# Reordering the first transfers of an eight-core decoder-block kernel, and splitting the last tile's output stage into two halves of its tokens

## The chip, the cores and the metric

The kernel runs on the 8 cores of one Trainium2 chip. Each core works on one sequence of the batch of 8 and shares nothing with the others. The metric is device microseconds (us) of the slowest core.

In the profiles PE is TensorE (matmuls) and PEld its weight loads, DVE is VectorE, ACT is ScalarE, POOL is GpSimd, SP is SyncE, which issues most of the transfers; a q behind a name means the engine's sequencer. Cores 0 to 3 are one die of the chip, 4 to 7 the other; two neighbouring cores such as 2 and 3 are called a pair.

Executions come in two states. In the slow state the cores of one die, sometimes of both, have a lower granted clock in the records and the time is some per cent longer; this happens to both kernels and says nothing about them. A fast execution is **undisturbed** when every core's mean granted clock was above 0.985.

## The reference

```python
D_MODEL = 1024; BATCH = 8; SEQ = 4096; D_FF = 2816; EPS = 1e-6

def ada_rmsnorm(x, g, shift, scale):          # shift, scale: one vector per sequence
    return rmsnorm(x, g) * (1.0 + scale[:, None, :]) + shift[:, None, :]

def swiglu_ffn(h, w_in, w_out):
    gate, up = jnp.split(h @ w_in, 2, axis=-1)
    return (jax.nn.silu(gate) * up) @ w_out

def reference(x, c, w_mod, b_mod, ...):
    c_act = jax.nn.silu(c)
    mod = c_act @ w_mod[l] + b_mod[l]          # 9 vectors of 1024: shift, scale, gate of 3 sub-layers
    ...
    h = ada_rmsnorm(x, g_ffn1, sh1, sc1)
    x = x + 0.5 * gt1 * swiglu_ffn(h, w_ffn1_in, w_ffn1_out)
    h = ada_rmsnorm(x, g_mix, sh2, sc2)
    x = x + gt2 * mixing(h)                    # convolution group and recurrence group
    h = ada_rmsnorm(x, g_ffn2, sh3, sc3)
    x = x + 0.5 * gt3 * swiglu_ffn(h, w_ffn2_in, w_ffn2_out)
    return ada_rmsnorm(x, g_final, f_shift, f_scale)
```

All arrays are float32; the matrix products of the kernel are in bf16.

## The kernel before

A core's sequence is cut into 8 tiles of 512 tokens and held with features on the partitions, so a tile is 8 chunks of 128x512. Phase 1 does FFN 1 for pairs of tiles and stores the result. Phase 2 does mixing, FFN 2, the final norm and the store of `y`, tile by tile. Weights travel as slabs of 0.5 MB into a pool of 10 slots. In the first pair the 22 input slabs (`w1i`) are cast from f32 to bf16 by a GpSimd DMA on the way in and written back to a scratch copy in HBM, which later pairs load.

The program is a list of operations. A small list scheduler in Python, which simulates the engines with estimated durations, fixes one static order for each engine; at run time every engine goes through its list in order and waits for semaphores. Three arguments matter below: `prio` (smaller first), `after` (an order for the scheduler only, no wait on the chip) and `sync` (a real semaphore wait). All operations of one kind come from one helper, so the profile gives all matmuls line 443, all activations 401, all DMAs 450.

The parts that the change touches:

```python
def load_slab(nm, r, cast, prio=None, after=()):
    b = new(sl, f"{nm}{r}")
    if cast:
        src = dr(w_src[nm], r)
        dma("PL", lambda: b.ap, lambda: src, D_CAST, slot_sem(b, "PL"), [], [b], slab=True, prio=prio, after=after)
        d = scr[nm][r]
        dma("SP", lambda: d.ap, lambda: b.ap, D_SLAB, lambda: wb_sems[b.slot], [b], [d], prio=prio)
    # ... (else: load the bf16 slab from scratch)

P.prio = -24
mods(M_SC1, [None] * 8)        # 8 slabs of w_mod, each reduced on DVE against silu(c): scale of FFN 1
gs_op(M_SC1, V_G1)             # gs = g * (1 + scale)
P.prio = -20
mods(M_SH1, [None] * 8)        # shift of FFN 1

def norm(xs, msc, msh, after=(), prio=None):
    r = stats(xs, after, prio)             # squares, sums, two ones-matmuls on PE, r = 1/rms on ACT
    hb = []
    for f in range(8):
        t_ = new(p2, "nt")
        stt(lambda t_=t_: t_.ap, lambda f=f: xs[f].ap, gs[msc].ap[:, f:f + 1], lambda: r.ap, ALU.mult, ALU.mult,
            [xs[f], r, gs[msc]], [t_], after=after, prio=prio)                  # x * gs * r on DVE
        b = new(p1, "hb")
        # ... o, i = b, t_
        act(o, i, AF.Identity, [t_, modv[msh]], [b], dur=0.7, bias=modv[msh].ap[:, f:f + 1], prio=prio,
            alt=v_ts(o, i, modv[msh].ap[:, f:f + 1], ALU.add))                  # + shift, on ACT or DVE
        hb.append(b)
    return hb

# the pairs of phase 1
xss = [load_x(x_dr, t, prio=(-22 if t == 0 else -15) if pi == 0 else lp, after=prev_in[8 * (t % 2):8 * (t % 2) + 8]) for t in tiles]
hbs = [norm(xs, M_SC1, M_SH1, after=(last_in,), prio=300) for xs in xss]
for j in range(FC):
    slab = load_slab("w1i", j, pi == 0)
    ops = ffn_in(slab, hbs, hids, j)       # 8 + 8 matmuls per tile of the pair
    # ...
last_in = ops[-1]
# ... 12 output slabs, ffn_out per 3 of them, xmid stored

# the end of each tile in phase 2
for q in range(4):
    slabs = [load_slab("w2o", 3 * q + s, t == 0) for s in range(3)]
    ffn_out(slabs, q, [xs], [hid], gth[M_GT3])
r = stats(xs)
for f in range(8):
    b = xs[f]
    stt(...)                               # x * gs * r
    act(...)                               # + shift
    dma("PL", lambda d=d: d.ap, lambda b=b: b.ap, D_CHUNK, slot_sem(b, "PL"), [b], [d])   # y, from GpSimd

# the end of the program, on SP
replay(engs["SP"], h)
for smh, v in stores.items():
    h.wait_ge(smh.h, v)                    # every semaphore that a DMA ever raised
```

## Time and profile before

| | before |
|---|---|
| first runs, us | 2420.52, 2420.62, 2418.84 (and a slow one, 2465.01) |
| undisturbed runs in the later calls (chips 9, 5, 3), mean us | 2422.9, 2423.7, 2424.3 |
| span of the eight cores in the profiled run | 2409.5 to 2431.0 |
| time before the first FFN matmul (core 1) | 66.4 |
| last FFN matmul to the end (core 1) | about 23 |

The page of the profile, for the slowest core (core 1). The second line gives each engine's busy time, its share of the span and its instructions:

```profile
span 2431.0 us, 34520 instructions; the slowest of 8 cores (2409.5 to 2431.0 us)
...
PE 2317.3 (95%) x11168; PEld 1093.3 (45%) x11168; DVE 1180.9 (49%) x1975; ACT 920.8 (38%) x1394; POOL 115.1 (5%) x221
```

PE is the bound, but a 95% average hides where the other 5% lies. The windows view of before, core 1, cuts the span into stages; its first line names the columns:

```profile
core 1: us, PE busy (x) PEld busy (x) DVE busy (x) ACT busy (x) POOL busy (x), PEclk, DMA share, GB/s
0.00:66.40 66.40, 2.34 (x5) 0.45 (x5) 35.53 (x72) 23.38 (x35) 2.99 (x9) 1.00 0.98 270
66.40:220.00 153.60, 153.60 (x702) 69.20 (x703) 46.29 (x74) 33.24 (x55) 14.25 (x27) 1.00 0.96 207
220.00:240.00 20.00, 14.37 (x57) 5.96 (x56) 8.93 (x16) 8.33 (x13) 1.08 (x2) 0.83 0.96 282
240.00:2408.00 2168.00, 2146.43 (x10408) 1017.55 (x10405) 1083.32 (x1807) 847.24 (x1281) 92.47 (x175) 1.00 0.63 186
2408.00:2431.00 23.00, 0.60 (x3) 0.10 (x1) 6.83 (x10) 8.59 (x12) 4.31 (x8) 0.60 0.24 91
```

PE does almost nothing in the first 66.4 us, while the DMA engines are full (share 0.98): the head is a matter of which bytes come first. PE is then full. It stalls between 220 and 240. And it does almost nothing in the last 23 us, where DMA is mostly idle too (share 0.24): the tail is a chain of latencies.

What ends the head is in the timeline of before, core 1 (start, duration, engine, line, operation, tiles; in brackets the idle time before it and what ended that):

```profile
58.83 1.22 DVE L499 SCALAR_TENSOR_TENSOR sb_slab<-sb_slab,sb_crow 128x1024 f32<-128x1024 f32 x1 [1.77 <-DMA sb_slab<-wmod]
...
60.64 0.16 DVE L423 TENSOR_TENSOR sb_modv<-sb_modr,sb_vecs 128x8 f32<-128x8 f32 x1
60.72 8.03 DVE L419 SCALAR_TENSOR_TENSOR sb_c<-sb_c,sb_gs 128x512 f32<-128x512 f32 x12
60.90 7.34 ACT L401 ACTIVATE sb_h<-sb_c,sb_modv 128x512 bf16<-128x512 f32 x11 [9.56 <-DVE sb_modv L423]
...
66.40 8.94 PE L443 MATMUL ps<-sb_h,sb_slab 128*128 128x512 bf16 x30 [16.57 <-ACT sb_h L401]
```

The sixteenth and last modulation slab lands at 58.7 and its reduction starts at 58.83. Only then can the multiplies by `gs*r` and the activations run for the eight chunks, and PE begins at 66.40. In the records of DMA landings, x of tile 1 (2 MB) arrived from 33.4 to 47.3, ahead of the last six modulation slabs (48.6 to 58.7), though nothing needed it yet.

The stall near 228, from the PE timeline of the same core:

```profile
227.77 0.38 PE L443 MATMUL ps<-sb_h,sb_ones 128*128 128x512 bf16 x1
233.78 0.59 PE L443 MATMUL ps<-sb_h,sb_ones 128*128 128x512 bf16 x1 [5.63 <-DVE sb_h L423]
```

Matmuls with `sb_ones` sum squares over the partitions. Here they belong to tiles 2 and 3, whose x is still coming: PE's static order holds them in the middle of the first pair's work, so PE stands for 5.6 us.

And the tail, from the timeline of before, core 1:

```profile
2411.06 1.28 ACT L401 ACT_TABLE_LOAD   x1 [1.47 <-PE ps L443]
...
2413.13 0.63 ACT L401 ACTIVATE sb_c<-sb_c 128x512 f32<-128x512 f32 x1
2413.86 5.39 DVE L419 SCALAR_TENSOR_TENSOR sb_c<-sb_c,sb_gs 128x512 f32<-128x512 f32 x8 [3.41 <-ACT sb_c L401]
2414.71 5.36 ACT L401 ACTIVATE sb_c<-sb_c,sb_modv 128x512 f32<-128x512 f32 x8 [0.95 <-DVE sb_c L419]
2415.98 5.18 POOL L450 DMA_DIRECT2D y<-sb_c  x8 [104.39 <-ACT sb_c L401]
```

The last FFN matmul is at 2407.9. The reciprocal root is ready at 2413.8, the eight chunks are normalized and shifted one behind the other, and the eighth store is issued at 2420.6. But the span ends at 2431.0. The records of GpSimd, which the timeline does not print, show a DRAIN instruction of 10.18 us that begins with that last store and ends at 2430.8; it is there on all eight cores. The Trainium skill, "VectorE: DVE Perf Modes", section "The DRAIN you can't avoid", puts the DRAINs that the runtime adds around a kernel at about 12 ns on all engines. This one carries a line of the kernel, L862, where its last block begins, so it may be of another kind; it took some 850 times that, while SP's DRAIN at the same line took 0.01 us.

### The profile page before, as it was taken

How to read it: one execution, taken by the hardware profiler on the slowest of the kernel's cores; microseconds unless marked ns; L12 is line 12 of the kernel's file. 1: busy time of each engine (PE TensorE's matmuls, PEld its weight loads, DVE VectorE, ACT ScalarE, POOL GpSimd, SP SyncE). 2: the span in 40 equal slices, each digit the busy share in tenths (PEclk: the TensorE clock that was granted, in tenths of full speed). 3: DMA queues.
4: the chain of work that ended last, by engine and by line, in shares of the span. 5: the costliest groups of instructions: out<-in, count | busy, mean ns of one | idle time of the engine just before them, and what ended most of it. 6: DMA issues, size and time to landing. Idle time of an engine off the chain costs nothing.

```text
span 2431.0 us, 34520 instructions; the slowest of 8 cores (2409.5 to 2431.0 us)
## 1 busy us (share of the span) xinstructions
PE 2317.3 (95%) x11168; PEld 1093.3 (45%) x11168; DVE 1180.9 (49%) x1975; ACT 920.8 (38%) x1394; POOL 115.1 (5%) x221
## 2 busy tenths in 40 slices
PE   0999999999999999999899999999999999999996
PEld 0444444444444445454354454454454454454442
DVE  4513233523352337676285385484484574573322
ACT  2313111401130115556264364364364464473312
POOL 0100100010000000000000000000000000000000
PEclk9999999999999999999999999999999999999998
DMA  9899589768966755565976555555555555555551
GB/s 266 201 210 242 161 203 231 181 193 206 222 188 178 191 160 196 168 216 163 223 190 220 190 176 189 185 179 189 176 179 185 191 182 182 186 179 189 166 181 61
DMA packets 131711, 460.32 MB, mean 189 GB/s; under 512 B 16048, under 2 KB 16176, under 8 KB 130864
## 3 DMA queue, kind: packets, MB, share of 16 engines
q1 hardware_dynamic: 113184, 378.15, 48.8%
q0 software_dynamic: 18352, 79.97, 16.4%
q8 instruction: 94, 1.54, 0.3%
q14 instruction: 81, 0.66, 0.1%
HBM read 446.78 MB, written 79.69 MB: 217 GB/s over the span
## 4 chain that ended last, share of the span: by engine, by line
PE 84%; DMA 5%; SPq 4%; ACT 3%; issue 2%; DVE 2%; ACTq 0%; DVEq 0%; POOL 0%; POOLq 0%
PE ps L443 84%; SPq L450 4%; ACT sb_c L401 2%; DMA sb_c<-xmid 2%; DMA sb_c<-x 1%; DMA sb_slab<-wmod 1%; DMA sb_slab<-w2o 1%; DVE sb_c L734 0%; DVE sb_c L409 0%; ACT L401 0%; DVE sb_h L423 0%; ACT sb_h L401 0%; DVE sb_c L423 0%; DVE sb_c L419 0%; DVE sb_c L429 0%
## 5 line engine op out<-in xcount | busy, mean ns | idle before, releaser
L443 PE MATMUL ps<-sb_h,sb_slab 128*128 128x512 bf16 x9984 | 2176.7, 380 | 16.6 <-ACT sb_h L401 16.6
L443 PEld LDWEIGHTS ps<-sb_h,sb_slab 128*128 128x128 bf16 x9984 | 978.7, 98 | 1196.5 <-issue 28.0
L423 DVE TENSOR_TENSOR sb_h<-ps,sb_c 128x512 bf16<-128x512 f32 x352 | 240.7, 690 | 770.0 <-PE ps L443 728.3
L401 ACT ACTIVATE sb_c<-ps 128x512 f32<-128x512 f32 x400 | 237.7, 596 | 891.8 <-PE ps L443 891.4
L401 ACT ACTIVATE sb_c<-sb_c 128x512 f32<-128x512 f32 x332 | 204.4, 627 | 294.3 <-DVE sb_c L419 194.9
L401 ACT ACT_TABLE_LOAD x102 | 130.9, 1283 | 219.3 <-PE ps L443 195.9
L419 DVE SCALAR_TENSOR_TENSOR sb_c<-ps,sb_gth,sb_c 128x512 f32<-128x512 f32 x128 | 94.9, 749 | 216.6 <-PE ps L443 215.9
L423 DVE TENSOR_TENSOR sb_c<-sb_c 128x512 f32<-128x512 f32 x224 | 149.1, 687 | 88.3 <-ACT sb_c L401 85.8
L419 DVE SCALAR_TENSOR_TENSOR sb_c<-sb_c,sb_gs 128x512 f32<-128x512 f32 x256 | 173.5, 746 | 32.6 <-ACT sb_c L401 32.5
L443 PE MATMUL ps<-sb_ub,sb_slab 128*128 128x256 bf16 x1024 | 115.0, 273 | 4.9 <-DVE sb_c L409 4.4
L401 ACT ACTIVATE sb_h<-sb_c,sb_modv 128x512 bf16<-128x512 f32 x160 | 105.1, 716 | 20.5 <-DVE sb_c L419 10.3
L499 DVE SCALAR_TENSOR_TENSOR sb_slab<-sb_slab,sb_crow 128x1024 f32<-128x1024 f32 x88 | 107.0, 1217 | 11.9 <-DMA sb_slab<-wmod 11.3
L443 PEld LDWEIGHTS ps<-sb_ub,sb_slab 128*128 128x128 bf16 x1024 | 99.6, 98 | 21.9 <-issue 8.1
L443 PE MATMUL ps<-sb_h,sb_ones 128*128 128x512 bf16 x96 | 34.8, 391 | 71.6 <-DVE sb_h L423 71.0
L450 POOL DMA_DIRECT2D y<-sb_c x64 | 34.5, 540 | 1124.1 <-ACT sb_c L401 974.9
L423 DVE TENSOR_TENSOR sb_h<-sb_c 128x512 bf16<-128x512 f32 x96 | 65.3, 688 | 25.4 <-ACT sb_c L401 23.3
L419 DVE SCALAR_TENSOR_TENSOR sb_c<-sb_ux,sb_vecs,sb_c 128x512 f32<-128x512 f32 x96 | 69.5, 745 | 1.7
L419 DVE SCALAR_TENSOR_TENSOR sb_c<-ps,sb_modv,sb_c 128x512 f32<-128x512 f32 x64 | 47.9, 749 | 32.4 <-PE ps L443 32.4
L419 DVE SCALAR_TENSOR_TENSOR sb_ub<-sb_c,ps 64x256 bf16<-64x256 f32 x128 | 53.8, 420 | 15.1 <-PE ps L443 11.7
L450 POOL DMA_DIRECT2D xmid<-sb_c x64 | 34.8, 544 | 360.0 <-DVE sb_c L419 358.3
L401 ACT ACTIVATE sb_c<-sb_c,sb_lam 128x512 f32<-128x512 f32 x64 | 50.0, 821 | 0.5
L443 PEld LDWEIGHTS ps<-sb_h,sb_ones 128*128 128x128 bf16 x96 | 9.0, 98 | 88.8 <-issue 81.9
(51 smaller groups left out, 508.7 us busy)
## 6 DMA issues: line engine op xcount, KB each, us to landing
sb_slab<-b_w2i SPq DMA_DIRECT2D x176, 512.0 KB, 3.7
sb_slab<-wmod SPq DMA_DIRECT2D x88, 512.0 KB, 5.9
sb_slab<-b_w2o SPq DMA_DIRECT2D x84, 512.0 KB, 3.5
sb_slab<-b_w1i SPq DMA_DIRECT2D x66, 512.0 KB, 6.0
sb_slab<-b_win SPq DMA_DIRECT2D x64, 512.0 KB, 4.4
sb_slab<-b_dcw SPq DMA_DIRECT2D x64, 512.0 KB, 3.5
sb_slab<-b_w1o SPq DMA_DIRECT2D x36, 512.0 KB, 5.2
sb_c<-x SPq DMA_DIRECT2D x64, 256.0 KB, 10.7
```

The source lines that it names most:

```text
L401: return A("ACT", dur, lambda: (lambda o, i: (lambda h: [h.activation(out=o, in_=i, func=func, bias=bias, scale=scale)]))(out(), in_()), r ...
L419: return A("DVE", dur, lambda: (lambda o, a, b: (lambda h: [h.scalar_tensor_tensor(out=o, in0=a, scalar=scalar, in1=b, op0=op0, op1=op1)]) ...
L423: return A("DVE", dur, lambda: (lambda o, a, b: (lambda h: [h.tensor_tensor(out=o, in0=a, in1=b, op=op)]))(out(), in0(), in1()), reads, wr ...
L443: return [h.matmul(o, lhsT=l, rhs=r, start=(first and i == 0), stop=(last and i == n - 1)) for i, (l, r) in enumerate(pr)]
L450: lambda: (lambda o, i: (lambda h: [h.dma_start(out=o, in_=i)]))(out(), in_()),
L499: return lambda h: [h.scalar_tensor_tensor(out=w, in0=w, scalar=1.0, in1=crow.ap, op0=ALU.mult, op1=ALU.mult, accum_out=o)]
```

## The change

Two independent parts.

The **head**: x of tile 0 goes first, then the sixteen modulation slabs of FFN 1, then x of tile 1. Casts 0 and 1 of `w1i` wait for modulation reductions, cast 2 for the fourth chunk of x of tile 1, and casts from 3 on for its last chunk. The norm is regrouped, so that DVE multiplies x by r (which needs no modulation) and ACT applies scale and shift in one activation. The first matmul group is split per chunk, so that it starts with the first chunk. The mixer's gate weights are loaded later, and so are the eight modulation slabs of FFN 1's gate, whose place moves from behind the second `w1i` slab to behind the ninth (not in the cuts below).

The **tail**: the last tile does its output matmuls, the sum of squares, the final norm and its stores for the first 256 tokens and then for the other 256, and issues those stores from SP instead of GpSimd. This costs twelve more loads of output slabs.

```diff
-        def load_slab(nm, r, cast, prio=None, after=()):
+        def load_slab(nm, r, cast, prio=None, after=(), sync=()):
 # ... sync goes to the cast's dma; mods() returns its last reduction and records all in mod_ops
-                stt(lambda t_=t_: t_.ap, lambda f=f: xs[f].ap, gs[msc].ap[:, f:f + 1], lambda: r.ap, ALU.mult, ALU.mult,
-                    [xs[f], r, gs[msc]], [t_], after=after, prio=prio)
+                tt(lambda t_=t_: t_.ap, lambda f=f: xs[f].ap, lambda: r.ap, ALU.mult, [xs[f], r], [t_], prio=prio, after=after)
 # ...
-                act(o, i, AF.Identity, [t_, modv[msh]], [b], dur=0.7, bias=modv[msh].ap[:, f:f + 1], prio=prio,
-                    alt=v_ts(o, i, modv[msh].ap[:, f:f + 1], ALU.add))
+                act(o, i, AF.Identity, [t_, modv[msh], gs[msc]], [b], dur=0.72, bias=modv[msh].ap[:, f:f + 1],
+                    scale=gs[msc].ap[:, f:f + 1], prio=prio,
+                    alt=v_ts(o, i, gs[msc].ap[:, f:f + 1], ALU.mult, modv[msh].ap[:, f:f + 1], ALU.add))
 # ... ffn_in(split=True): the gate group's 8 matmuls as 8 operations; ffn_out and stats take a width
-            xss = [load_x(x_dr, t, prio=(-22 if t == 0 else -15) if pi == 0 else lp, after=prev_in[8 * (t % 2):8 * (t % 2) + 8]) for t in tiles]
-            hbs = [norm(xs, M_SC1, M_SH1, after=(last_in,), prio=300) for xs in xss]
+            if pi == 0:
+                xss = [load_x(x_dr, t, prio=-26 if t == 0 else -15, after=[None if t == 0 else sh1_last] * 8) for t in tiles]
+                hbs = [norm(xs, M_SC1, M_SH1, prio=-23 if t == 0 else 300) for t, xs in zip(tiles, xss)]
 # ... (else: as before)
-                slab = load_slab("w1i", j, pi == 0)
-                ops = ffn_in(slab, hbs, hids, j)
+                slab = load_slab("w1i", j, pi == 0, sync=() if pi else (mod_ops[M_SH1 + 2 * j] if j < 2 else xss[-1][3 if j == 2 else 7].lw,),
+                                 after=[xb.lw for xb in xss[-1]] if pi == 0 and j >= 2 else ())
+                ops = ffn_in(slab, hbs, hids, j, split=(j == 0))
 # ...
+            last = t == n_tiles - 1
+            for cs in ([slice(0, T)] if not last else [slice(0, T // 2), slice(T // 2, T)]):
+                # ... the four groups of ffn_out, stats, final norm on w = 256 columns
+                    e = "SP" if last else "PL"
+                    dma(e, lambda d=d: d.ap, o, D_CHUNK * w / T, slot_sem(b, e), [b], [d])
 # ...
-        loads.sort(key=lambda o: use[o.writes[0]])
+        loads.sort(key=lambda o: (min(o.prio, 0), use[o.writes[0]]))
```

## The prediction

> **What bounds it now.** The page gives PE 95% of a 2431.0 us span, at 0.99 of its clock. The windows put 2.3 us of PE work into the first 66.4 us and 0.6 into the last 23; in between PE idles about 27 us of 2342. So the steady part is PE-bound (0.217 us per 512-column matmul); the change attacks the 66 us head and the 23 us tail.
>
> **Head before.** The timeline shows the sixteenth modulation slab (scale and shift of FFN 1) landing at 58.7, because x of tile 1 (2 MB) and four weight casts went before it with DMA saturated (share 0.98, 270 GB/s). Then come the last reduction and eight chained multiply/activation pairs (0.67 us each) before the first matmul at 66.4.
>
> After: constants (landing 7.5 as now), x of tile 0 (0.86 us per chunk: done near 15), sixteen slabs (1.63 us each in the trace: near 41, near 45 with two casts let in). The multiply by 1/rms no longer needs the modulation, so only activations remain behind it, and the first group starts per chunk. First FFN matmul estimated at 47-49, about 18 us earlier.
>
> Not all stays won. Until x of tile 1 has landed (about 54) and is normalized (61-65), PE has only tile 0: about 3.4 us per slab, with casts 2 and up held behind x of tile 1, landing from about 57. I expect about 5 us of starvation, plus a cold restart (first matmuls take 0.43 us; the Trainium skill, "TensorE: Matmul & The Clock Gate", Part 1, says PE falls to half clock after an idle window of about 3.4 us; the trace agrees: slow after the head and after the 5.6 us gap at 228). Net head gain about 13 us. From 100 to 240 us DMA share is about 1.0 and x of tile 3 lands at 236, where PE already waits 5.6 us. PE will arrive there earlier than DMA can, so I take off 3 us: 10 remain.
>
> **Tail before.** Timeline: last FFN matmul 2407.9, reciprocal root ready 2413.8 (with a 1.28 us table load), last store issued 2420.6, landed 2423.9, end 2431.0. The GpSimd drain behind the last store takes 10.2 us on every core, and ends the span.
>
> After: half the columns, table already loaded: root ready 2.8 us after the last matmul, eight chunks 3.5-4 us, stores from SP, so the GpSimd drain runs long before. SP then walks about 120 semaphore waits at 0.05 us. End about 13.5 us after the last matmul instead of 23.4. Halving costs PE little (256-column matmuls are 0.110 us), but twelve more 0.5 MB slabs are loaded: 24 at 1.6 us each in 39 us, just enough with 9 prefetched; perhaps 1 us lost. Tail gain about 9.5 us.
>
> **Elsewhere.** DVE 0.746 becomes 0.69 per norm multiply; off the path.
>
> **Prediction.** 2420.6 - 10 - 9.5 = about 2401 us; range 2391 to 2411. Faster by over 2% (48 us) exceeds what head and tail can give: 0.01. Within 2%: 0.98. Slower: 0.01.
>
> **What would show it.** First FFN matmul before 50; a PE gap of several us between 53 and 66 ending on a DMA or on the activations of tile 1; casts landing from about 57; wait on stats of tiles 2/3 near 210-225 as long as before or longer; last matmul to end 13-15 us; no GpSimd drain in the end chain.
>
> **What would make it wrong.** Casts held so late that PE starves through several slabs (head gain under 5); casts arriving so smoothly that all 18 us stay (2393); the stall near x of tile 3 growing to 15 us; slab starvation in the last tile; a rearranged static order moving the mid-kernel gaps.

## The result

The fast runs of the changed kernel took 2407.28, 2410.0 and 2412.54 us, against 2420.52, 2420.62 and 2418.84 before. A ratio is computed as the mean time of one kernel's fast runs over that of the other's of the same rounds, so it is not quite the ratio of the medians. Here it is 0.9958, with a 95% interval of 0.9936 to 0.9981: faster by about 10 us. Three of the changed kernel's six runs fell in the slow state and are left out.

The page of after, for its slowest core (core 0):

```profile
span 2405.7 us, 35029 instructions; the slowest of 8 cores (2386.8 to 2405.7 us)
...
PE 2318.5 (96%) x11346; PEld 1110.4 (46%) x11346; DVE 1183.6 (49%) x2019; ACT 931.4 (39%) x1394; POOL 111.2 (5%) x213
```

PE's busy time is the same within 1.2 us. What changed lies in its idle time. The windows of after, core 0, cut at the corresponding places (columns as above):

```profile
0.00:45.70 45.70, 1.17 (x2) 0.21 (x2) 31.77 (x68) 11.16 (x16) 1.42 (x6) 1.00 0.95 281
45.70:62.00 16.30, 10.57 (x38) 4.15 (x39) 9.31 (x17) 10.04 (x15) 3.71 (x7) 0.92 1.03 238
62.00:210.00 148.00, 148.00 (x678) 66.65 (x677) 46.14 (x74) 34.70 (x57) 12.19 (x23) 0.99 1.00 217
210.00:230.00 20.00, 16.86 (x71) 7.26 (x70) 11.19 (x19) 10.85 (x17) 1.08 (x2) 0.91 1.00 330
230.00:2391.00 2161.00, 2141.68 (x10562) 1032.06 (x10559) 1081.12 (x1836) 859.82 (x1283) 92.85 (x175) 1.00 0.64 190
2391.00:2405.70 14.70, 0.27 (x1) 0.10 (x1) 4.06 (x11) 4.86 (x10) 0.00 (x0) 0.61 0.22 72
```

The head is 20.7 us shorter and the tail 8.3 us shorter, but a new stage with 5.7 us of idle PE has appeared behind the head (16.30 less 10.57), and the stall near x of tile 3 is still there (20.00 less 16.86 is 3.1 us idle, against 20.00 less 14.37, 5.6, before). The end of the head, in the timeline of after, core 0:

```profile
43.20 1.23 DVE L500 SCALAR_TENSOR_TENSOR sb_slab<-sb_slab,sb_crow 128x1024 f32<-128x1024 f32 x1 [2.07 <-DMA sb_slab<-wmod]
...
44.54 0.17 DVE L423 TENSOR_TENSOR sb_modv<-sb_modr,sb_vecs 128x8 f32<-128x8 f32 x1
44.81 2.22 ACT L401 ACTIVATE sb_h<-sb_c,sb_modv,sb_gs 128x512 bf16<-128x512 f32 x3 [24.88 <-DVE sb_modv L423]
```

The sixteenth slab now lands at 43.05, and 2.6 us after its reduction began PE starts. The PE timeline of after shows the start and the new gap:

```profile
45.76 8.73 PE L443 MATMUL ps<-sb_h,sb_slab 128*128 128x512 bf16 x32 [28.68 <-ACT sb_h L401]
54.33 0.38 PE L443 MATMUL ps<-sb_h,sb_ones 128*128 128x512 bf16 x1
57.48 0.38 PE L443 MATMUL ps<-sb_h,sb_ones 128*128 128x512 bf16 x1 [2.77 <-DVE sb_h L423]
60.76 19.47 PE L443 MATMUL ps<-sb_h,sb_slab 128*128 128x512 bf16 x77 [2.90 <-DMA sb_slab<-w1i]
```

With two slabs cast, PE does 32 matmuls of tile 0, then waits 2.8 us for the squares of tile 1 and 2.9 us for the third slab, which landed at 60.6. Later, in the same view of after:

```profile
215.61 0.38 PE L443 MATMUL ps<-sb_h,sb_ones 128*128 128x512 bf16 x1
219.13 0.38 PE L443 MATMUL ps<-sb_h,sb_ones 128*128 128x512 bf16 x1 [3.14 <-DVE sb_h L423]
```

And the tail, in the timeline of after, core 0:

```profile
2393.07 0.47 ACT L401 ACTIVATE sb_c<-ps,sb_cst 128x256 f32<-128x256 f32 x1 [1.11 <-PE ps L443]
2393.64 0.42 ACT L401 ACTIVATE sb_c<-sb_c 128x256 f32<-128x256 f32 x1
2394.16 2.77 DVE L423 TENSOR_TENSOR sb_c<-sb_c 128x256 f32<-128x256 f32 x8 [1.60 <-ACT sb_c L401]
2394.67 3.55 ACT L401 ACTIVATE sb_c<-sb_c,sb_modv,sb_gs 128x256 f32<-128x256 f32 x7 [0.62 <-DVE sb_c L423]
2395.34 3.77 SPq L450 DMA_DIRECT2D y<-sb_c  x8
```

No table load and no long GpSimd DRAIN at the end any more: in the records that DRAIN now begins at 2293, a hundred microseconds before the end, and still lasts 10.7 us (10.3 to 11.5 over the eight cores). The last store is issued at 2398.72 and lands at 2400.50. SP does not stand still for that landing: its records show 121 closing semaphore waits, about 0.05 us apart, from 2399.16 to 2405.49, with a single pause of 0.35 us.

One profile is one core of one execution, so I also read from each trace, as a mean over its fully recorded cores (in e1_again below without core 3, which had the lower clock), when the n-th matmul with weights was executed. The 352nd is past the head, the 760th is past the stall at x of tile 3:

| us, mean of cores | 1st | 352nd | 760th | last | last to end |
|---|---|---|---|---|---|
| before | 66.3 | 144.1 | 238.6 | 2396.5 | 23.4 |
| after | 45.1 | 132.1 | 227.2 | 2385.1 | 15.2 |

From the 760th to the last matmul both take 2158 us (2157.9 and 2158.0): in these two executions the middle of the kernel neither wins nor loses, and everything is in the head and in the tail. (Over all the traces below this stretch runs from 2154.7 to 2163.7, so a difference of a few us in it needs more than one trace.)

### The profile page after: what moved, and what is told of

Same layout as the page of the kernel before. It is cut to its first block, busy times and chain, and to the rows that moved or that the text cites. A ratio compares the mean times of both kernels' runs of the same rounds, so it can differ in the third digit from the quotient of the medians.

```text
span 2405.7 us, 35029 instructions; the slowest of 8 cores (2386.8 to 2405.7 us)
## 1 busy us (share of the span) xinstructions
PE 2318.5 (96%) x11346; PEld 1110.4 (46%) x11346; DVE 1183.6 (49%) x2019; ACT 931.4 (39%) x1394; POOL 111.2 (5%) x213
## 4 chain that ended last, share of the span: by engine, by line
PE 87%; DMA 6%; ACT 3%; DVE 2%; issue 2%; SPq 1%; ACTq 0%; DVEq 0%; POOLq 0%
PE ps L443 87%; DMA sb_c<-x 2%; ACT sb_c L401 2%; DMA sb_c<-xmid 2%; SPq L450 1%; DMA sb_slab<-wmod 1%; DVE sb_c L423 1%; DMA sb_slab<-w1i 0%; DVE sb_c L749 0%; DVE sb_c L409 0%; ACT L401 0%; DVE sb_h L423 0%; DVE sb_c L419 0%; DVE sb_ub L419 0%; DVE sb_c L429 0%
## 5 line engine op out<-in xcount | busy, mean ns | idle before, releaser
L443 PE MATMUL ps<-sb_h,sb_slab 128*128 128x512 bf16 (+1 forms) x10160 | 2178.2, 376 | 31.8 <-ACT sb_h L401 28.9
L443 PEld LDWEIGHTS ps<-sb_h,sb_slab 128*128 128x128 bf16 x10160 | 995.9, 98 | 1195.9 <-issue 44.6
L423 DVE TENSOR_TENSOR sb_c<-sb_c 128x512 f32<-128x512 f32 (+1 forms) x492 | 308.8, 672 | 115.6 <-ACT sb_c L401 113.0
L401 ACT ACTIVATE sb_c<-sb_c 128x512 f32<-128x512 f32 (+1 forms) x329 | 198.5, 616 | 263.0 <-DVE sb_c L419 183.3
L419 DVE SCALAR_TENSOR_TENSOR sb_c<-ps,sb_gth,sb_c 128x512 f32<-128x512 f32 (+1 forms) x136 | 96.7, 717 | 212.0 <-PE ps L443 211.6
L401 ACT ACTIVATE sb_h<-sb_c,sb_modv,sb_gs 128x512 bf16<-128x512 f32 x151 | 108.9, 801 | 38.5 <-DVE sb_modv L423 24.9
L423 DVE TENSOR_TENSOR sb_h<-sb_c 128x512 bf16<-128x512 f32 (+1 forms) x98 | 65.8, 678 | 21.8 <-ACT sb_c L401 19.6
L443 PE MATMUL ps<-sb_h,sb_ones 128*128 128x512 bf16 (+1 forms) x98 | 34.4, 382 | 37.3 <-DVE sb_h L423 37.0
L419 DVE SCALAR_TENSOR_TENSOR sb_ub<-sb_c,ps 64x256 bf16<-64x256 f32 x128 | 53.8, 420 | 15.1 <-PE ps L443 11.6
L409 DVE TENSOR_SCALAR sb_c<-ps,sb_vecs 64x256 f32<-64x256 f32 x85 | 40.7, 484 | 8.9 <-ACT sb_c L401 4.7
L401 ACT ACTIVATE sb_c<-sb_c,sb_modv,sb_gs 128x512 f32<-128x512 f32 (+1 forms) x65 | 43.6, 751 | 1.2 <-DVE sb_c L423 1.2
```

The lines of the kernel that those rows point to most:

```text
L401: return A("ACT", dur, lambda: (lambda o, i: (lambda h: [h.activation(out=o, in_=i, func=func, bias=bias, scale=scale)]))(out(), in_()), r ...
L409: f = lambda: (lambda o, a: (lambda h: [h.tensor_scalar(out=o, in0=a, scalar1=s1, scalar2=s2, op0=op0, op1=op1)]))(out(), in0())
L419: return A("DVE", dur, lambda: (lambda o, a, b: (lambda h: [h.scalar_tensor_tensor(out=o, in0=a, scalar=scalar, in1=b, op0=op0, op1=op1)]) ...
L423: return A("DVE", dur, lambda: (lambda o, a, b: (lambda h: [h.tensor_tensor(out=o, in0=a, in1=b, op=op)]))(out(), in0(), in1()), reads, wr ...
L443: return [h.matmul(o, lhsT=l, rhs=r, start=(first and i == 0), stop=(last and i == n - 1)) for i, (l, r) in enumerate(pr)]
```

## The experiments

The question is small: the prediction was 2401 us, the fast runs took about 2410. Two candidate reasons: either the head gives back more than I took off (at the new gap, or at x of tile 3), or the tail was mis-sized. Twelve runs were made, two of them of the change unaltered, on three chips, each call with its own runs of before. "Mean core" is the mean span over the cores of the undisturbed runs; it scatters less than the slowest core does (standard deviation from run to run 0.8 to 2.5 us), so a difference of 1 us in the last column is not resolved.

| run | chip | ratio of fast runs [95%] | undisturbed: us (runs) | before, same chip | mean core less before's |
|---|---|---|---|---|---|
| e1_again | 9 | 1.0004 [0.9973, 1.0035] | 2411.3 (2 of 6) | 2422.9 | -12.5 |
| e2_head_only | 9 | 1.0018 [0.9979, 1.0056] | 2418.4 (3 of 6) | 2422.9 | -4.7 |
| e3_tail_only | 9 | 0.9974 [0.9959, 0.999] | 2416.9 (5 of 6) | 2422.9 | -5.4 |
| e4_sp_stores | 9 | 0.9987 [0.997, 1.0004] | 2420.3 (4 of 7) | 2422.9 | -2.4 |
| e5_warm | 5 | 0.9941 [0.9929, 0.9954] | 2409.6 (5 of 6) | 2423.7 | -13.1 |
| e6_no_hold | 5 | 0.9952 [0.9938, 0.9967] | 2412.3 (5 of 6) | 2423.7 | -11.9 |
| e7_order_only | 5 | 0.9948 [0.9935, 0.9962] | 2409.9 (5 of 6) | 2423.7 | -14.2 |
| e8_waits | 5 | 0.9931 [0.9917, 0.9944] | 2407.0 (4 of 6) | 2423.7 | -16.4 |
| e9_late_stats | 3 | 0.9916 [0.9888, 0.9944] | 2406.4 (6 of 6) | 2424.3 | -18.2 |
| e10_combo | 3 | 0.9888 [0.986, 0.9916] | 2399.8 (6 of 6) | 2424.3 | -24.8 |
| e11_control | 3 | 0.9938 [0.9903, 0.9973] | 2411.7 (4 of 7) | 2424.3 | -13.0 |
| e12_best | 3 | 0.9854 [0.9819, 0.9889] | 2391.3 (5 of 6) | 2424.3 | -30.2 |

The runs that are missing from the fourth column were slow or had a pair of cores at a lower clock. All twelve gave correct results. The times of the matmuls in the traces:

| us, mean of cores | 1st | 352nd | 760th | 352nd to 760th | last to end |
|---|---|---|---|---|---|
| e1_again | 44.7 | 131.7 | 227.0 | 95.4 | 15.2 |
| e2_head_only | 43.8 | 132.1 | 228.2 | 96.1 | 23.4 |
| e3_tail_only | 65.0 | 143.1 | 236.3 | 93.2 | 15.8 |
| e4_sp_stores | 65.5 | 143.4 | 234.0 | 90.6 | 20.3 |
| e5_warm | 45.0 | 130.8 | 227.9 | 97.1 | 15.2 |
| e6_no_hold | 44.7 | 128.7 | 226.0 | 97.2 | 15.2 |
| e7_order_only | 47.1 | 131.5 | 224.2 | 92.8 | 15.4 |
| e8_waits | 45.6 | 131.8 | 225.8 | 94.0 | 10.5 |
| e9_late_stats | 45.4 | 131.4 | 219.5 | 88.1 | 15.7 |
| e10_combo | 44.7 | 130.7 | 218.8 | 88.1 | 10.7 |
| e11_control | 44.8 | 131.5 | 226.7 | 95.1 | 15.2 |
| e12_best | 47.5 | 132.1 | 220.2 | 88.1 | 11.3 |

### e1_again: the change unaltered, timed in rounds

No edit.

> The changed kernel unaltered, timed again with more rounds and with the per-core spans of both kernels. Theory A (the traces are right: about 11.5 us won by the head and 8.3 us by the tail on every core, so the mean core is about 20 us shorter; the 10 us first timed come from few fast runs and from the slowest of eight cores, which scatters by 10 us): mean core span 18 to 21 us below that of the kernel before, slowest core 13 to 22 us below, ratio about 0.992 to 0.9945. Theory B (half of the gain is given back in the middle of the kernel, where the static order was rearranged, and the profiled run of the kernel before was an unusually slow one): ratio stays at 0.9955 to 0.9965 and the mean core span is only about 10 us shorter.

The ratio of fast runs is 1.0004, which seems to say that the change is worth nothing. The cores say otherwise. In four of the six runs two neighbouring cores (2 and 3, or 6 and 7, or 0 and 1) have a mean clock of 0.98 and a span 20 to 30 us longer than the rest. In the profiled run these are cores 2 and 3, at 0.983 and 0.981, with spans of 2421.5 and 2429.5 us; the other six take 2390.2 to 2407.2. The windows view of e1_again, core 3 (columns as above):

```profile
77.00:215.00 138.00, 138.00 (x527) 57.18 (x526) 33.15 (x52) 20.32 (x34) 10.55 (x20) 0.81 0.92 211
```

and the same stretch of the same execution on core 4:

```profile
77.00:215.00 138.00, 137.37 (x629) 62.54 (x640) 43.84 (x69) 29.37 (x50) 12.13 (x23) 1.00 1.00 228
```

Core 3 does 527 matmuls where core 4 does 629, with PE busy all the time on both: its clock was granted at 0.81. In the clock records the value is 0.8125, for 162 us, beginning 4.2 us after the clock had come back from the half-rate window behind the head (4.8 us on core 2). The Trainium skill, "TensorE: Matmul & The Clock Gate", Part 1, section "Seeing it yourself", describes a limiter that takes a whole die to 13/16 of its clock while three or more of its cores run dense matmuls, and holds it there. The level agrees (13/16 is 0.8125). The extent does not: here it is a pair, for 162 us, and in undisturbed runs all eight cores run dense matmuls at a mean clock of 0.99.

With the pair's runs set aside, two runs remain: 2411.3 against 2422.9 us, and a mean core 12.5 us shorter. Neither theory had that: it is far below the 18 to 21 us of theory A, which took the two first traces at their word, and little above the 10 us of theory B. Is the pair's lower clock a cost of the change, since its head is followed by a half-clock window in the gap at 54 to 61? On this chip it looked so: four of six runs here, three in e2_head_only, none in ten runs of before. But on chip 5, four kernels with the new head showed no such pair in their fast runs, two of them (e7_order_only, e8_waits) with the same half-clock window; and on chip 3 one run of before had it (2444.72 us, cores 2 and 3 at 0.982 and 0.983). So the change is not needed for it. What brings it on stays open.

### e2_head_only and e3_tail_only: one part at a time

```diff
 # e2_head_only: the change, but
-            last = t == n_tiles - 1
+            last = False
```

```diff
 # e3_tail_only: before, but with the change's stats, ffn_out and end of the tile
+            last = t == n_tiles - 1
+            for cs in ([slice(0, T)] if not last else [slice(0, T // 2), slice(T // 2, T)]):
+                # ... ffn_out, stats, final norm and SP stores per half, as in the change
```

> Only the head part (order of transfers, held casts, norm without the scale in its multiply, per-chunk first group); the last tile in one piece, stored by GpSimd. Theory A: first FFN matmul near 44.7 us, 352nd slab matmul about 12 us earlier than in the kernel before, last matmul to end 23.4 us as before; time 11 to 12 us below before (ratio 0.9953). Theory B: the head is won, but the middle gives back about as much, so the ratio is 0.998 or nearer to 1 and the distance from the 1056th to the last matmul grows by 5 us or more.

> Only the tail part (last tile in two halves, stores from SP) on the kernel before. Theory A: first FFN matmul near 66 us as before, last matmul to end 15.1 us in place of 23.4 us, time 8 us below before (ratio 0.9966). Theory B (the tail is worth less, because the second set of output slabs or the half-width matmuls slow PE): last matmul about 3 us or more later than in the kernel before, ratio 0.998 or nearer to 1.

In the times, the head alone takes 4.7 us off the mean core and the tail alone 5.4; together 10.2, against 12.5 to 13.0 for the whole change. Both are below what theory A of their expectations had (11 to 12 us and 8 us off the slowest core, where 4.5 and 6.0 came). The two parts add up, roughly, as parts at the two ends of a program should. In the traces, the tail alone has the old head (1st matmul at 65.0) and the new end (15.8), and the head alone the new head (43.8) and the old end (23.4).

The traces also give sizes, larger ones. Over the three kernels with the old head (before, e3, e4) the 352nd matmul is at 143.5 on average, and over four with the new one (after, e1, e2, e11) at 131.8: the head wins 11.7 us by then. At the 760th it is 236.3 against 227.3: 9.0. So 2.7 us are given back between the two, at x of tile 3. The last chunk of that x lands at 232.4 before and 222.2 after (mean over the cores); it did not become earlier by as much as PE did. The 2.7 is no firmer than its traces: from the 352nd to the 760th the three with the old head take 94.5, 93.2 and 90.6 us.

In the tail, last matmul to end falls from 23.4 to 15.2, which is 8.2 us, but the last matmul itself comes later: from the 10000th to the last it is 218.0 us before and 219.4 after (218.0 in e2, which has the old end, and 219.4 in e3). Halving costs 1.4 us on PE. Net 6.8.

The sum of 9.0 and 6.8 is 15.8, and the timed gain is 11.6 to 13.0. The record says where most of the other 3 us are likely to lie: in traces of executions that were long or short for their kernel. Against the undisturbed timed mean of its own kernel, the profiled mean core was 6.4 us long in before (2420.4 against 2414.0), 2.3 in e3 and 0.9 in e4; in e2 it was 1.2 long, in e11 1.6 short and in after 3.5 short. Before's trace is thus the least typical, and x of tile 3 landed latest in it. Taking instead, of these, the two traces nearest to their timed means, e4 for the old head and e2 for the new, the 352nd matmul moves from 143.4 to 132.1, which is 11.3 us, but the 760th only from 234.0 to 228.2, which is 5.8: 5.5 us are given back there, not 2.7, and the head's 5.8 is near its timed 4.7. So 9.0 and 2.7 are the favourable reading. The head is worth 5 to 9 us and the tail 5.4 (timed) to 6.8 (traces); single traces do not settle it more closely.

### e4_sp_stores: only the engine that issues the last stores

```diff
 # before, but
-                dma("PL", lambda d=d: d.ap, lambda b=b: b.ap, D_CHUNK, slot_sem(b, "PL"), [b], [d])
+                e = "SP" if t == n_tiles - 1 else "PL"
+                dma(e, lambda d=d: d.ap, lambda b=b: b.ap, D_CHUNK, slot_sem(b, e), [b], [d])
```

> The kernel before with one edit: the eight stores of the last tile are issued by SP in place of GpSimd; no halves. If the GpSimd drain (10.2 us behind its last store) ends the span: it now runs long before, and the end is SP's, about 7 us after its last issue (about 120 waits of 0.05 us that come behind the last issue), so last matmul to end falls from 23.4 to about 20 us, and the time by about 3.5 us (ratio 0.9985). If rather the landing of the stores ends the span, less than 1 us is won. What is left to the 15.1 us of the full change, about 5 us, is then the halves' (half-width chain, no table load).

The tail becomes 20.3 instead of 23.4 us, and the mean core 2.4 us shorter (3.5 us were expected). The timeline of e4_sp_stores, core 3, whose span is 2420.0:

```profile
2407.59 4.96 SPq L450 DMA_DIRECT2D y<-sb_c  x8
```

In the records the last of these stores is issued at 2412.22 and lands at 2414.46, and SP is through its closing waits at 2419.75: the long DRAIN is off the chain, but the waits have taken its place. So the DRAIN was worth 3 us, not 10, because the next thing in line was nearly as long. The rest of the tail's 8.2 us is then left to the halves and the table that is already loaded; no run separates these two.

### e5_warm: fill the gap behind the head

```diff
 # the change, and
+        def warm(n, op, hb):
+            bank = new(ps, "wm")
+            A("PE", mm_us(n), ..., [ones, hb], [bank], prio=299, after=(op,))   # n matmuls that nobody reads
 # ...
+                if pi == 0 and j == 1:
+                    warm(12, ops[0], hbs[0][0])
+                    warm(12, stat_mm[1], hbs[0][0])
```

> The changed kernel with 24 idle matmuls (result thrown away) put where PE waits in the head: twelve before the second statistics matmul of tile 1, twelve before slab 2. They fill the two gaps of about 3 us, wait for nothing new and move no other instruction in PE's order. First: no half-clock window near 60 us, so the 352nd slab matmul comes about 2.5 us earlier than in the changed kernel (132 to about 129.5). Second, the clock: in the earlier runs of kernels with the new head, in about half of the executions one pair of neighbouring cores (0/1, 2/3, 4/5 or 6/7) was granted 0.81 of the clock for 162 us, from 4 to 5 us after PE had come back from that half-clock window. Theory H (the second cold-to-full step, taken by all cores within a few us, sets it off): no pair at 0.98 mean clock in six executions, ratio 0.990 to 0.992. Theory R (the dense work simply starts earlier, or chance): pairs at 0.98 stay as frequent, about 2 to 4 of six.

The dummy matmuls keep PE busy where it would have idled. The PE timeline of e5_warm, core 3:

```profile
52.99 2.75 PE L595 MATMUL ps<-sb_h,sb_ones 128*128 128x512 bf16 x12
55.58 0.38 PE L443 MATMUL ps<-sb_h,sb_ones 128*128 128x512 bf16 x1
56.93 0.38 PE L443 MATMUL ps<-sb_h,sb_ones 128*128 128x512 bf16 x1 [0.97 <-DVE sb_h L423]
57.15 2.75 PE L595 MATMUL ps<-sb_h,sb_ones 128*128 128x512 bf16 x12
61.57 3.83 PE L443 MATMUL ps<-sb_h,sb_slab 128*128 128x512 bf16 x17 [1.67 <-DMA sb_slab<-w1i]
```

The idle time before the 110th microsecond falls from about 6 to 1.8 us, but real work is no earlier by as much: the 352nd matmul comes 1 us sooner (I had expected 2.5, a miss), and the 760th not at all. The clock records of e5_warm have no half-clock window between 52 and 216 us, so the half clock behind the gap is worth about 1 us here, and at x of tile 3 even that is gone. No pair of cores at a lower clock appeared, but the unwarmed kernels on this chip had none either, so theory H of the clock is not tested by this run.

### e6_no_hold: casts not held behind x of tile 1

```diff
 # the change, but
-                slab = load_slab("w1i", j, pi == 0, sync=() if pi else (mod_ops[M_SH1 + 2 * j] if j < 2 else xss[-1][3 if j == 2 else 7].lw,),
-                                 after=[xb.lw for xb in xss[-1]] if pi == 0 and j >= 2 else ())
+                slab = load_slab("w1i", j, pi == 0, sync=(mod_ops[M_SH1 + 2 * j],) if pi == 0 and j < 2 else ())
```

> The changed kernel without the holding of casts 2 and up behind x of tile 1 (casts 0 and 1 keep their wait). PE's order then holds 120 slab matmuls of tile 0 before the statistics of tile 1. If holding is what helps (theory A): casts take DMA time from the last modulation slabs and from x of tile 1, the first FFN matmul comes 1 to 4 us later and x of tile 1 lands later than 60 us, and the 352nd slab matmul comes later than 132 us by 2 us or more. If holding is what starves PE (theory C): the first matmul stays within 2 us, the gap between 54 and 61 us goes, no half-clock window follows, and the 352nd comes 3 us or more earlier than 132. Under theory H of the clock, no gap also means no pair of cores at 0.98.

The PE timeline of e6_no_hold, core 3:

```profile
46.41 26.96 PE L443 MATMUL ps<-sb_h,sb_slab 128*128 128x512 bf16 x112 [30.10 <-ACT sb_h L401]
74.05 1.89 PE L443 MATMUL ps<-sb_h,sb_slab 128*128 128x512 bf16 x8 [0.68 <-DMA sb_slab<-w1i]
```

The gap is gone: with casts arriving, PE does 112 matmuls of tile 0 without a pause. The price is that x of tile 1 lands at 75.4 instead of 53.5. The Trainium skill, "DMA: Bandwidth & Descriptors", section "Issuing engines are not separate DMA queues", says that transfers started by different engines run on the same 16 engines and interleave; the DMA share of about 1.0 in this stage and the 22 us that GpSimd's casts cost SP's loads agree. The 352nd matmul is about 3 us earlier than in the change and its like (128.7 against 131.5 to 132.1), as theory C had it, but the 760th only about 1 us (226.0), and the time is no better than that of its neighbours (2412.3, against 2409.6 and 2409.9). So the hold itself is close to neutral: it decides which of two waits PE has, as long as DMA is full until x of tile 3.

### e7_order_only: the order of transfers alone

```diff
 # the change, but norm as before, and
-                ops = ffn_in(slab, hbs, hids, j, split=(j == 0))
+                ops = ffn_in(slab, hbs, hids, j, split=False)
```

> The changed kernel with the old norm (scale inside the DVE multiply, so the eight multiplies wait for the modulation) and the old single first group; order of transfers, holds and tail as changed. Theory A (DMA sets the start of the dense phase: PE's early matmuls only wait again at x of tile 1): first FFN matmul near 50 instead of 44.7 us, but the 352nd slab matmul later by only 0 to 2 us, since the gap after tile 0 shrinks by what the start loses. Rival: the 5 us are lost in full, the 352nd comes at 136 to 137 us.

The first matmul moves from 45 to 47.1 (50 were expected), and nothing else becomes later: the 352nd is at 131.5. The PE timeline of e7_order_only, core 4:

```profile
62.15 5.71 PE L443 MATMUL ps<-sb_h,sb_slab 128*128 128x512 bf16 x13 [3.84 <-DMA sb_slab<-w1i]
```

It starts 2 us later and runs into the same wait for the same slab at about 61 to 62. So the regrouped norm and the split first group only lengthen the gap that follows. The head's gain is the order of the transfers, with the holds and the moved loads that belong to it.

### e8_waits: who does the closing waits

```diff
 # the change, but
                 replay(engs["SP"], h)
                 for smh, v in stores.items():
-                    h.wait_ge(smh.h, v)
+                    if smh in tail_sems:              # the last tile's stores: 17 waits
+                        h.wait_ge(smh.h, v)
 # ...
                 replay(engs["PL"], h)                 # GpSimd, long finished by then
+                for smh, v in stores.items():
+                    if smh not in tail_sems:
+                        h.wait_ge(smh.h, v)
```

> The changed kernel, with the closing waits for all transfers other than the last tile's stores made by GpSimd (idle for 100 us by then) instead of SP behind its last store. No transfer goes unwaited. If SP's walk through about 120 waits sets the end of the changed kernel: last matmul to end falls from 15.1 to 10 to 11 us, nothing else moves, and undisturbed cores end 4 to 5 us earlier. If the landing of the last stores sets it: under 1 us.

The tail falls from 15.2 to 10.5 us. On e8_waits, core 0, whose span is 2402.8, the last store is issued at 2400.41, lands at 2402.18, and the end is at 2402.77. The records show 16 waits on SP there in place of 121, still about 0.05 us apart, with one pause of 0.89 us that ends with that landing. So the 105 waits that are gone, for semaphores that had been satisfied for long, took about 5.2 us; of these 4.7 are won, because the landing, which SP's walk had covered, is now in the chain. On chip 5 this run has the best time of its four (2407.0 us).

### e9_late_stats: squares of the next pair later in PE's order

```diff
 # the change, but
-                hbs = [norm(xs, M_SC1, M_SH1, after=(last_in,), prio=300) for xs in xss]
+                hbs = [norm(xs, M_SC1, M_SH1, after=(stats_gate,), prio=300) for xs in xss]
 # ...
                 ops = ffn_out(slabs, q, xss, hids, gth[M_GT1])
+                stats_gate = ops[-1] if q == 1 else stats_gate
```

> The changed kernel with one edit in the first FFN: the statistics of the next pair of tiles are ordered behind the second quarter of the output matmuls in place of behind the last input matmul; PE no longer meets them before x of tile 3 has landed (about 224 to 236 us). Theory A (part of what the head wins is given back at about 215 us, where PE waits in its order for the statistics of tile 3 while DMA is full): no gap and no half-clock window near 215 us, the distance from the 352nd to the 760th slab matmul falls from about 95 to 89 or 90 us, undisturbed mean core 4 to 6 us shorter than the control of the same job. Rival: PE then waits at the start of the second pair for its normed tiles, and the 1056th matmul comes no earlier than in the control (291 us).

The statistics of the next pair are now placed behind half of the output matmuls of this one, so x of tiles 2 and 3 has time to land. PE's timeline of e9_late_stats, core 0, around the place of the stall:

```profile
189.76 55.42 PE L443 MATMUL ps<-sb_h,sb_slab 128*128 128x512 bf16 x256
```

One unbroken row of 256 matmuls from 190 to 245. From the 352nd to the 760th it takes 88.1 us instead of 95.1, and the mean core is 5.2 us shorter than in e11_control on the same chip. (In the two traces the 760th matmul is 7.2 us earlier than the control's and the last one only 2.0, within the scatter of the stretch between; the 5.2 rests on the timed runs.) This is the term that the head had lost to: what PE wins at the start it can keep only if its order does not ask for x of tile 3 so early.

### e10_combo, e11_control and e12_best

```diff
 # e10_combo: e6_no_hold, e8_waits and e9_late_stats together
 # e11_control: the change unaltered, on this chip
 # e12_best: e10_combo, and the same delay in phase 2
-            hb = norm(xs, M_SC2, M_SH2, prio=940 if t > 1 else MIX0 - 10 + t)
+            hb = norm(xs, M_SC2, M_SH2, prio=940 if t > 1 else MIX0 - 10 + t, after=(out_anchor[t - 2],) if t > 1 else ())
 # ... (out_anchor[t]: the last matmul of tile t's second output group)
```

> The changed kernel again, unaltered, as the control on the same chip as its variants. Undisturbed executions: ratio to the kernel before 0.9945 to 0.996, mean core 12 to 14 us shorter. Executions in which a pair of cores has a clock of 0.98 are counted; on one chip they were 4 of 6, on another none of 20 of its relatives.

> Late statistics, no holding of casts, and the closing waits moved to GpSimd, together. Without the hold alone, the 352nd slab matmul came at 128.7 us against 132, but the 760th at 226 against 227, and the time was no better. If the wait for tile 3 ate those 3 us: the 760th now comes at 217 to 220 us, last matmul to end is 10.5 us, mean undisturbed core 11 to 13 us shorter than the control. If the casts that run ahead only move the DMA shortage to another place: the 1056th comes no more than 5 us earlier than the control's.

> As the combination, and in the second half of the kernel the statistics of tile t (t of 2 and more) are ordered behind the second quarter of the output matmuls of tile t-2, as the trace shows PE waiting there 1.5 to 5 us at nearly every tile, 10 to 15 us in all. If these waits are only early placement: gaps in the middle fall under 6 us and the mean core is another 5 to 9 us shorter than the combination. Rival: the mixing of tile t starts later and DVE's long chain then holds PE, and it is no faster or slower than the combination.

The control repeats the change's gain on a third chip: 2411.7 against 2424.3 us undisturbed, a mean core 13.0 us shorter than before's. The combination takes another 11.8 off the control's mean core, of which e9's part is 5.2, the closing waits about 5, and the lifted hold the remaining 1 to 2. Lifting the hold pays here, where it paid nothing alone (e6), since nothing takes the gain away at x of tile 3 any more; this split rests on differences between runs, and the last part is near what they can resolve.

e12_best is the fastest: 2391.3 us against 2424.3 before and 2411.7 for the change, 5.4 us less on the mean core than e10_combo, as expected. Where it comes from is in the middle: from the 760th to the last matmul 2154.7 us instead of 2161.7 in e10_combo. That stretch alone does not show it, since e7_order_only has 2154.9 without this edit; but within it the three thousands of matmuls 6000 to 7000 and 8000 to 10000 take 611.7 us in e12_best, 619.8 in e10_combo and at least 617.8 in every other trace (stretches picked after seeing the traces). My expectation that the gaps of the middle would fall below 6 us was a miss; the sum of PE's gaps over 0.5 us is 10.6, against 13.8 in e10_combo.

## Why the prediction was right, point by point

In short: the mechanism held at both ends, and the size did not hold as well. Of 19.5 us predicted, 11.6 to 13.0 came. The verdict within 2% was safe, since no gain under 48 us could break it; the time stayed in the range because the range was 10 us wide to each side.

- **Range.** Within 2%, as predicted; the runs at 2407 to 2412 lie in and just above the range of 2391 to 2411, to the slow side of the 2401. The undisturbed gain is 11.6 us (chip 9) and 12.6 (chip 3), where 19.5 were predicted. By the timed single parts both terms were too large: the head alone gave 4.7 us off the mean core instead of 10, the tail alone 5.4 instead of 9.5.
- **The end of the head.** "First FFN matmul estimated at 47-49, about 18 us earlier": 45.1 instead of 66.3, 21 us earlier. The reason was right: the landing of the sixteenth slab (43.05 instead of 58.7) sets it. The use of the regrouped norm is not: with the old norm (e7_order_only) the first matmul is 2 us later and the 352nd not at all.
- **Starvation behind it.** "I expect about 5 us of starvation": 6.3 us of PE gaps before the 110th microsecond. "Net head gain about 13 us": 11.7 at the 352nd matmul. That this is so near is partly luck: the start came 3 us earlier than predicted, and 9 us instead of 5 were lost behind it. The cold restart that I had named as an extra is worth about 1 us (e5_warm).
- **Given back at x of tile 3.** "I take off 3 us: 10 remain": the place was right, the size is open: 2.7 given back and 9.0 left over seven traces, 5.5 and 5.8 over the two most typical ones, 4.7 left in the timed runs of the head alone. e9_late_stats shows that this is the place: with the statistics later in PE's order, the stall and the loss are gone.
- **The tail.** "End about 13.5 us after the last matmul instead of 23.4 ... perhaps 1 us lost ... Tail gain about 9.5 us": this term was mis-sized too. It is 15.2 instead of 13.5, and 1.4 us are lost on PE, so 6.8 us are gained in the traces and 5.4 in the timed runs. On core 0 of after the parts are 3.2 us to the root (2.8 predicted), 4.7 from there to the issue of the last store (3.5 to 4), and 6.8 from that issue until SP is through its waits (6 for 120 waits). The landing of the store, 1.8 us after its issue, is hidden behind these waits. The mechanism held: no GpSimd DRAIN at the end (e4_sp_stores), SP's waits in its place (e8_waits).
- **What remains.** Head and tail as measured in the traces give 15.8 us, and the times give 11.6 to 13.0. Most of these 3 us probably come from before's long and after's short trace; that is argued from their means and not shown. I did not foresee the pair of cores at 0.98 either, which made four of six runs of the change (and three of six of its head alone) on one chip as slow as before or slower; its cause is open.

## What to carry to other kernels

Moving work earlier at the start pays only as far as the next wait whose end does not move with it; look for that wait (here x of tile 3, asked for by a statistic in PE's static order), and move the demand there too: that was worth as much as the head's whole timed gain. At the end of a program, follow the last chain past the last store: what the closing engine still has to do, its drain and its waits, can be as long as the arithmetic, and taking away one of them only brings out the next. When a per cent matters, look at each core's clock in each run before believing a ratio.

## What the Trainium skill lacked or had wrong

- "TensorE: Matmul & The Clock Gate", Part 1, "Seeing it yourself": the 13/16 limiter is told as taking a whole die soon after a third core on it runs dense matmuls, for as long as the load lasts. Slow runs here look like that (in one, four cores of one die at 0.814 to 0.815 and 2871.76 us), but undisturbed runs keep eight cores dense at a clock of 0.99 for 2.3 ms. And a third form is not told: a pair of neighbouring cores at 0.8125 for 162 us, beginning 4 to 5 us after a half-clock window.
- The same page, Part 1, "What's actually happening", calls the clock ratio binary (4/8 or 8/8); the records here show 0.8125 as well, as the page's later section itself allows.
- "VectorE: DVE Perf Modes", "The DRAIN you can't avoid": two kinds of DRAIN are told, a flush after each DVE operation and the runtime's own of about 12 ns on all engines. The DRAINs that the kernel's last block brings fit neither: 0.01 us on SP, 5.11 us on DVE in before (it ends with DVE's last multiply), and on GpSimd 10.18 us from the last store it issued, or 10.3 to 11.5 us where that was a hundred microseconds before the end.
- No page that I found gives the cost of a wait for a semaphore that is already satisfied (the nearest, in "Advanced Engine Details and Errata", is about reading a semaphore's value): in SP's records they follow each other every 0.05 us (121 from 2399.16 to 2405.49 in the change), and taking 105 of them away won 4.7 us (e8_waits).
